# Eight loads of the second half of x tied to the end of the first half's RWKV-7 projections, in a hybrid RWKV-7 / RG-LRU / GLA block

## The chip, the core and the metric

The kernel runs on one core of one Trainium2 chip. The metric is device microseconds of one execution; before the change the median of three runs is 1198.15 us. TensorE (PE) does the matmuls, VectorE (DVE), ScalarE (ACT) and GpSimd (POOL) the elementwise work, and SyncE (SP) only issues DMAs. Each engine takes its instructions strictly in the order in which they stand in its row, so an instruction that waits holds up all that stand behind it.

## The reference, cut to what matters

T = 1024 tokens, width D = 1024, one layer. One combined projection feeds three mixers, whose outputs go through an output projection and then an FFN.

```python
hn = rms_norm(x, norm1_g)                       # x * rsqrt(mean(x*x) + eps) * g
p_rw, p_lru, p_gla = split(hn @ w_in)           # RWKV-7 | RG-LRU | GLA
y_rw  = rwkv7_mixer(p_rw)     # p + (token_shift(p) - p) * mu, then a delta-rule scan
y_lru = rglru_mixer(p_lru)    # causal conv of width 4, gates, a linear recurrence
y_gla = gla_mixer(p_gla)      # chunked gated linear attention, rms_norm * silu(gate)
x = x + concat([y_rw, y_lru, y_gla]) @ w_out
x = x + (silu(rms_norm(x) @ w_gate) * (rms_norm(x) @ w_up)) @ w_down
return rms_norm(x)
```

## The kernel before

All is kept transposed: channels on the 128 partitions, tokens along the free axis. The tokens are taken as two halves of 512 (h = 0 and 1). For each half a tile `y0` or `y1` (128 x 8 x 515) first holds x (eight slices k of 128 channels, in columns 3 to 514) and later the mixers' outputs. Columns 0 to 2 of a slice are room for the convolution's three earlier tokens.

**Projections.** `mm3` computes one projection tile of 128 outputs x 512 tokens with 24 matmuls in one PSUM bank `mm`, of which there are two. Weights come as two pieces `wr` of 256 KB (L120), which ACT and DVE split in a high and a low part (`wh` L104, `wl` L105); both are written back to DRAM (`parts`, L122, L123), so that half 1 loads them instead of making them again. x is split alike into `xh`, `xl`. The result leaves PSUM by DVE L252, which multiplies it with `rstd`, the norm's factor. `proj` can therefore run its matmuls before `rstd` is there, but only as far as there are `mm` banks.

**rstd of half 1** is made by `split_x(1)`: squares of the eight slices of y1 (L225), their sum over channels by one matmul (L174 into a bank `pi`), then on ACT `Ln` (L136) and `Exp` (L137). ACT must load a table (ACT_TABLE_LOAD) each time it goes from `Exp` to `Ln` or back.

**Token shift.** `rw_shift` keeps the last token of each of half 0's eight RWKV-7 projections in a column of `carry` (128 x 8), with one ACT copy each (L276); half 1 takes its first token from there. The eight projections are steps R0 (seven of them) and H0 (the eighth, `pgl`).

**What sets the order.** A list of steps (ORDER) is written out in the program: R0, H0, then pieces of the RWKV-7 chain (a, b, c, p), of GLA (P0, G0), of RG-LRU (l, L) and, in the middle, X1 (`load_x(1)`), S1 (`split_x(1)`) and R1, half 1's projections. A scheduler then merges the steps by priorities (AHEAD lifts some of them) and by its own estimate of when operands are ready, and writes each engine's row for good. A single added dependency can so move rows on all engines.

**Names the prediction uses.** Half 0's GLA step G0 ends with L574 (copies out of PSUM), L584 to L586 (gate), L593, L174 into `px`, twice L595 (`Ln`) and L597 (`Exp`). RG-LRU's step L01 begins beside it with L619, L611, L621 (gate), L628 and L630 (convolution), L634 (matmul into `px`, two banks) and L635 (ACT out of `px`). L455 and L465 are small matmuls of the RWKV-7 chain, L301 and L309 of its preparation.

Of the kernel before, what the change touches and what calls it, by code (L numbers as in the profile page):

```python
# [68 lines left out]
def hybrid_block(tc, xT, vec, cst, w_in, w_gk, w_ups, lru_w, gk_up, w_out, w_gu, w_dn, outT):  # L69
    nc = tc.nc  # L70
    V, G, S, PE = nc.vector, nc.gpsimd, nc.scalar, nc.tensor

    with ExitStack() as ctx:
# [12 lines left out]
        carry = cp.tile([P, 8], F32, name="carry")  # L86
# [125 lines left out]

        def load_x(h, ks=range(NK)):
            x = ys[h]
            for k in ks:
                nc.sync.dma_start(out=x[:, k, 3:], in_=xT[k, :, h * HT : (h + 1) * HT])

# [494 lines left out]
        with tc.high_priority(offset=10000):  # L712
            S.dma_start(out=vt, in_=vec)
            pre = [[load_w(w_in[6, :, 0:4], 6, 0)]]
            load_x(0, range(2))
            with tc.high_priority(offset=-500):
                pre.append([load_w(w_in[2, :, 0:4], 2, 0)])
            load_x(0, range(2, 4))
            with tc.high_priority(offset=-500):
                pre[0].append(load_w(w_in[6, :, 4:8], 6, 1))  # L720
            load_x(0, range(4, NK))
            nc.sync.dma_start(out=ct[:, CST["ones"][0] :], in_=cst[:, CST["ones"][0] :])
            xs = split_x(0)
# [363 lines left out]
        for f in range(PRE, NF):  # L1087
# [5 lines left out]
            h = gate_up(f, f + 1 if f < NF - 1 else None)  # L1093
# [253 lines left out]
```

## Time and profile before

| | |
|---|---|
| median of three runs (lowest, highest) | 1198.15 us (1198.10, 1199.42) |
| the profiled execution, its time | 1197.18 us |
| its span, granted clock of TensorE | 1195.4 us, 0.996 |
| TensorE busy | 1158.2 us (97%) |
| VectorE, ScalarE, GpSimd busy | 817.2 (68%), 558.5 (47%), 179.5 (15%) |
| DMA | 225.52 MB, 189 GB/s over the span |

TensorE is busy for all but some 37 us of the span, so what moves the time is mostly what puts a hole in its row or closes one. The profiled execution is 0.97 us under the median, and 1.8 us of its time lie outside the span.

### The profile page before, as it was taken

What the parts mean: (1) busy time and instruction counts of PE and PEld (TensorE: products, weight loads), DVE (VectorE), ACT (ScalarE), POOL (GpSimd) and SP (SyncE); (2) the same over time, 40 slices, a digit from 0 to 9 for tenths busy, and PEclk for the clock granted to TensorE, in tenths of its full rate; (3) what the DMA queues carried; (4) which work ended last, traced back from release to release, by engine and by line L of the source; (5) the groups of instructions that cost most, each with busy time, mean ns of one, the idle gap of its engine ahead of it and who ended that gap; (6) DMA issues with size and microseconds to landing.
All of it is one profiled execution on the core that took longest, in us unless ns stands there. A gap on an engine that the chain in (4) does not pass through costs nothing.

```text
span 1195.4 us, 18422 instructions
## 1 busy us (share of the span) xinstructions
PE 1158.2 (97%) x6550; PEld 906.2 (76%) x6550; DVE 817.2 (68%) x1513; ACT 558.5 (47%) x972; POOL 179.5 (15%) x141
## 2 busy tenths in 40 slices
PE   8899999999999999988999999999999999999996
PEld 5676667677776777766788788888888878888886
DVE  6878797887759687468978654356665465555675
ACT  7445734864551367546433333333333344444552
POOL 0000000000000000000026544455545400000000
PEclk9999999999999999999999999999999999999998
DMA  9865444253433269783699862245545798665322
GB/s 320 300 223 193 142 148 134 90 158 98 142 109 104 67 206 313 249 312 116 219 337 326 283 213 82 89 132 185 170 152 167 277 358 293 194 194 168 116 98 71
DMA packets 125212, 225.52 MB, mean 189 GB/s; under 512 B 13984, under 2 KB 17344, under 8 KB 125120
## 3 DMA queue, kind: packets, MB, share of 16 engines
q1 hardware_dynamic: 124432, 223.78, 56.0%
q8 instruction: 51, 0.84, 0.3%
q10 hardware_dynamic: 688, 0.57, 0.1%
q14 instruction: 41, 0.34, 0.1%
HBM read 149.84 MB, written 74.45 MB: 188 GB/s over the span
## 4 chain that ended last, share of the span: by engine, by line
PE 65%; DVE 14%; DMA 9%; ACT 8%; issue 3%; SPq 1%; POOL 0%; DVEq 0%; ACTq 0%; POOLq 0%
PE mm L869 24%; PE mm L1132 18%; PE mm L133 15%; DMA wr<-w_gu_dram 3%; DVE x L862 2%; DMA x<-w_dn_dram 2%; PE pi L368 1%; DMA wr<-w_in_dram 1%; DVE ws L862 1%; DMA wd<-x 1%; PE pi L408 1%; ACT L663 1%; DMA parts<-wh 1%; DVE wl L105 1%; DVE x L831 1%
## 5 line engine op out<-in xcount | busy, mean ns | idle before, releaser
L133 PE MATMUL mm<-xl,wh 128*128 128x512 f32 x420 | 168.8, 402 | 0.0
L133 PE MATMUL mm<-xh,wh 128*128 128x512 f32 x400 | 162.6, 407 | 3.9 <-ACT wh L104 3.1
L133 PE MATMUL mm<-xh,wl 128*128 128x512 f32 x400 | 162.9, 408 | 0.3 <-DVE wl L105 0.3
L104 ACT CAST wh<-wr 128x512 fp32r<-128x512 f32 x133 | 82.0, 619 | 123.1 <-PE mm L869 43.4
L104 ACT CAST vh<-wr 128x512 fp32r<-128x512 f32 x81 | 50.2, 622 | 103.7 <-PE mm L1132 39.1
L133 PEld LDWEIGHTS mm<-xl,wh 128*128 128x128 f32 x420 | 78.9, 188 | 21.9 <-issue 6.1
L133 PEld LDWEIGHTS mm<-xh,wh 128*128 128x128 f32 x400 | 75.1, 188 | 26.8 <-issue 5.9
L133 PEld LDWEIGHTS mm<-xh,wl 128*128 128x128 f32 x400 | 75.1, 188 | 22.6 <-issue 5.8
L105 POOL TENSOR_TENSOR wl<-wr,wh 128x512 fp32r<-128x512 f32 x36 | 51.1, 1418 | 268.1 <-DVE x L1042 208.1
L1132 PE MATMUL mm<-ft,vh 128*128 128x512 f32 x264 | 81.5, 389 | 0.0
L1132 PE MATMUL mm<-ft,wh 128*128 128x512 f32 x264 | 81.4, 389 | 0.0
L862 DVE TENSOR_TENSOR x<-x 128x512 f32<-128x512 f32 x71 | 58.7, 834 | 29.5 <-DMA x<-w_dn_dram 16.9
L105 DVE TENSOR_TENSOR wl<-wr,wh 128x512 fp32r<-128x512 f32 x97 | 66.2, 685 | 7.0 <-ACT wh L104 6.6
L417 POOL MEMSET ri<- 128x256 f32 x8 | 2.5, 312 | 390.0 <-DVE ri L402 387.9
L1132 PEld LDWEIGHTS mm<-ft,vh 128*128 128x128 f32 x264 | 49.5, 188 | 10.6 <-DVE ft L105 0.3
L1132 PEld LDWEIGHTS mm<-ft,wh 128*128 128x128 f32 x264 | 49.5, 188 | 10.5 <-DVE ft L105 0.2
L105 POOL TENSOR_TENSOR vl<-wr,vh 128x512 fp32r<-128x512 f32 x36 | 49.5, 1375 | 37.9 <-ACT vh L104 34.9
L1132 PE MATMUL mm<-ft,wl 128*128 128x512 f32 x132 | 51.4, 389 | 0.0
L1132 PE MATMUL mm<-ft,vl 128*128 128x512 f32 x132 | 51.4, 389 | 0.0
L105 POOL TENSOR_TENSOR vl<-ws,vh 128x512 fp32r<-128x512 f32 x27 | 38.3, 1420 | 39.6 <-ACT vh L104 34.8
L104 ACT CAST wh<-ws 128x512 fp32r<-128x512 f32 x33 | 20.4, 622 | 50.9 <-PE mm L869 43.7
L105 POOL TENSOR_TENSOR wl<-ws,wh 128x512 fp32r<-128x512 f32 x27 | 36.9, 1367 | 36.4 <-ACT wh L104 35.0
(501 smaller groups left out, 2898.4 us busy)
## 6 DMA issues: line engine op xcount, KB each, us to landing
wr<-w_gu_dram SPq DMA_DIRECT2D x108, 256.0 KB, 3.1
parts<-wh SPq DMA_DIRECT2D x60, 256.0 KB, 3.3
parts<-wl SPq DMA_DIRECT2D x60, 256.0 KB, 3.0
wh<-parts SPq DMA_DIRECT2D x57, 256.0 KB, 2.7
wl<-parts SPq DMA_DIRECT2D x57, 256.0 KB, 2.9
wr<-w_in_dram SPq DMA_DIRECT2D x44, 256.0 KB, 3.7
x<-w_dn_dram SPq DMA_DIRECT2D x44, 256.0 KB, 4.7
wd<-x SPq DMA_DIRECT2D x44, 256.0 KB, 4.3
```

Of the source, the lines that this page charges most:

```text
L104: S.copy(out=hi, in_=src)
L105: lo_eng.tensor_tensor(out=lo, in0=src, in1=hi.bitcast(F32), op=ALU.subtract)
L133: PE.matmul(out=ps, lhsT=ww[:, kk], rhs=xx(k), start=first, stop=last)
L368: PE.matmul(out=pgs[hh][:, n * P : n * P + P], lhsT=BKn[hs(hh), nn, 64 * hh : 64 * hh + 128], rhs=ARn[hs(hh), nn], start=True, stop=True)
L408: PE.matmul(out=ps[hs(hh), n * w : n * w + w], lhsT=lhs(hh, n), rhs=rhs(hh, n), start=True, stop=True)
L417: G.memset(hi(Zt), 0.0)
L663: S.activation(out=gate, in_=gate, func=AF.Exp, scale=-0.5)
L831: V.scalar_tensor_tensor(out=xk, in0=xk, scalar=vc("g2", k), in1=rs, op0=ALU.mult, op1=ALU.mult)
L862: eng.tensor_tensor(out=out, in0=a, in1=b, op=op)
L869: PE.matmul(out=ps, lhsT=ww[:, kk], rhs=xx, start=first and kk + i == 0, stop=kk == len(xc) - 1 and i == 2, skip_group_check=True)
L1132: PE.matmul(out=out(m), lhsT=ww[:, m], rhs=xx, start=first and open_(m) and k + i == 0, stop=k == KF - 1 and i == 2, skip_group_check=True)
```

## The change

`load_x(h)` for h = 1 gets one ACT copy ahead of its loads. It writes the eight columns of `carry` into column 3 of y1's eight slices. The eight loads then overwrite column 3, among others, with x. What the copy writes is thus never read; but each load must come after the copy, and the copy after the last of the eight writes to `carry`, which is that of step H0. (Line numbers from L216 on are higher by 3 after the change.)

```diff
         def load_x(h, ks=range(NK)):
             x = ys[h]
+            if h:
+
+                S.copy(out=x[:, :, 3], in_=carry)
             for k in ks:
                 nc.sync.dma_start(out=x[:, k, 3:], in_=xT[k, :, h * HT : (h + 1) * HT])
```

On SP's row the eight loads (`y1`, 256 KB each) stood early, among the weights (`wr`) of the first projections and the write-backs (`parts`). Before:

```order
L120 DMA wr<-w_in_dram 128x512
L181 DMA gku<-gk_up_dram 32x128
L216 DMA y_101<-xT_dram 128x512 x2
L189 DMA rt<-w_gk_dram 128x128
L216 DMA y_101<-xT_dram 128x512 x2
L122 DMA parts<-wh 128x512
L216 DMA y_101<-xT_dram 128x512
L123 DMA parts<-wl 128x512
```

After, on the same row, some fifty places further on:

```order
L122 DMA parts_81<-wh_699 128x512
L219 DMA y1_101<-xT_dram 128x512
L123 DMA parts_81<-wl_700 128x512
L120 DMA wr_1014<-w_in_dram 128x512
L219 DMA y1_101<-xT_dram 128x512
L122 DMA parts_81<-wh_719 128x512
L123 DMA parts_81<-wl_720 128x512
L120 DMA wr_1036<-w_in_dram 128x512
L219 DMA y1_101<-xT_dram 128x512 x6
```

All eight loads now stand behind thirteen more weight pieces than before, six of them in one run.

On ACT's row, at the end of GLA's half 0, `rstd` of half 1 is made by L136 and L137. Before (the names with u are work tiles of GLA and RG-LRU):

```order
L595 ACT_TABLE_LOAD
L595 ACTIVATE u_qk<-px,vt 128x512
L628 ACTIVATE u_2311<-y_100,vt 128x512
L619 ACTIVATE u_2304<-ga 128x512
L136 ACTIVATE rstd<-pi,vt 128x512
L137 ACT_TABLE_LOAD
L137 ACTIVATE rstd<-rstd 128x512
L621 ACTIVATE u_2304<-u_2304 128x512
L276 COPY carry<-pw 128x1
L595 ACT_TABLE_LOAD
```

After (L598 is L595 of before, L600 is L597, L622 is L619, L624 is L621, L631 is L628):

```order
L598 ACT_TABLE_LOAD
L598 ACTIVATE u_qk<-px,vt 128x512
L631 ACTIVATE u_2312<-y_100,vt 128x512
L598 ACTIVATE u_qk<-px,vt 128x512
L622 ACTIVATE u_2300<-ga 128x512
L600 ACT_TABLE_LOAD
L600 ACTIVATE u_qk<-u_qk 128x1024
L624 ACTIVATE u_2300<-u_2300 128x512
L136 ACT_TABLE_LOAD
L136 ACTIVATE rstd<-pi,vt 128x512
L137 ACT_TABLE_LOAD
L137 ACTIVATE rstd<-rstd 128x512
```

Both L595, both L621 and L597 now stand ahead of `rstd`, with a table load for L597 and one for L136 between.

On PE's row the third projection tile of half 1 begins at the 577th of the matmuls of L133. It writes the `mm` bank of the first tile, which DVE must have emptied with `rstd`. Before, it followed the second tile (`mm_2415`) at once:

```order
L174 MATMUL px_2145<-u_2_2143,ct_67 128x512
L450 MATMUL pc_2736<-R0_2744,Tt_1812 64x64 x4
L133 MATMUL mm_2415<-xh7_2268,wh_2432 128x512
L133 MATMUL mm_2415<-xl7_2269,wh_2432 128x512
L133 MATMUL mm_2415<-xh7_2268,wl_2433 128x512
L133 MATMUL mm_2454<-xh0_2240,wh_2455 128x512
L133 MATMUL mm_2454<-xl0_2241,wh_2455 128x512
```

After, other work stands between the second tile (`mm_2416`) and the third (`mm_2455`); L637 is L634 of before, L468 is L465 and L458 is L455 (the first rows of that work):

```order
L133 MATMUL mm_2416<-xh7_2269,wl_2434 128x512
L174 MATMUL pi_2296<-rt_2240,ct_67 128x512
L453 MATMUL pc_2737<-R0_2745,Tt_1813 64x64 x4
L637 MATMUL px_2318<-u_0_2312,lw_2310 128x512
L637 MATMUL px_2321<-u_0_2312,lw_2310 128x512
L468 MATMUL pp_2738<-XR0_1714,UV0_1080 64x64
L458 MATMUL pc_2737<-UV0_1080,BKt_1748 64x64
```

and its last rows, with the third tile's first:

```order
L468 MATMUL pp_2738<-XR1_1715,UV1_1081 64x64
L468 MATMUL pp_2738<-XR0_1714,UV0_1080 64x64
L468 MATMUL pp_2738<-XR1_1715,UV1_1081 64x64
L637 MATMUL px_2333<-u_1_2327,lw_2325 128x512
L133 MATMUL mm_2455<-xh0_2241,wh_2456 128x512
```

The three L637 and the L458/L468 group came after the third tile's first matmuls before, and the sum for `rstd` (L174 into `pi`) stood inside the second tile. The chain's small matmuls moved as well: the ends of GLA's scores and sums stand 12 matmuls of L133 later on PE's row than before (the last L578, now L581, after the 17th matmul of the second tile instead of after the 5th), and similar shifts of 12 to 22 run from about the 62nd matmul of L133 to the 570th. From about the 1300th on, and in the whole FFN, PE's row is the same.

## Rows read from the trace of the kernel before

**Rows 1.** Stretches: length, busy PE, PEld, DVE, ACT, POOL, granted clock, DMA share, GB/s.

```profile
18.00:45.00 27.00, 22.61 (x98) 15.63 (x98) 19.02 (x46) 18.44 (x35) 0.00 (x0) 1.00 0.89 318
40.00:60.00 20.00, 19.65 (x91) 15.54 (x92) 19.75 (x54) 5.76 (x13) 0.00 (x0) 1.00 0.88 304
```

**Rows 2.** TensorE's waits, 18 to 60 us: us in total, times, longest.

```profile
PE mm L133 <- ACT wh L104: 3.1, 2, 2.8
PE pi L301 <- ACT pw L279: 0.8, 1, 0.8
PE mm L133 <- DVE wl L105: 0.3, 1, 0.3
PE pi L174 <- ACT rt L320: 0.2, 1, 0.2
```

**Rows 3.** SyncE's queue, 17 to 33 us: start, us, line; last, its loads' landing time.

```profile
17.80 0.96 SPq L216 DMA_DIRECT2D y<-xT_dram  x2
...
23.95 1.62 SPq L120 DMA_DIRECT2D wr<-w_in_dram  x2
25.62 1.43 SPq L216 DMA_DIRECT2D y<-xT_dram  x3
...
y<-xT_dram SPq DMA_DIRECT2D x8, 256.0 KB, 4.8
```

**Rows 4.** TensorE's waits, 60 to 240 us, the three chain waits.

```profile
PE pi L301 <- DVE Tt L426: 1.1, 1, 1.1
PE pi L408 <- DVE ri L420: 1.0, 1, 1.0
PE pi L174 <- DVE rt L341: 0.8, 1, 0.8
```

**Rows 5.** ScalarE in order of time from 213 us: start, us, instruction, wait before it.

```profile
213.44 0.43 ACT L574 COPY u_v<-px 128x128 f32<-128x128 f32 x2 [7.33 <-PE px L572]
...
215.90 0.81 ACT L628 ACTIVATE u<-y,vt 128x512 f32<-128x512 f32 x1 [0.98 <-DVE y L586]
...
217.74 1.28 ACT L595 ACT_TABLE_LOAD   x1
219.03 0.69 ACT L595 ACTIVATE u_qk<-px,vt 128x512 f32<-128x512 f32 x1
...
220.32 0.62 ACT L619 ACTIVATE u<-ga 128x512 f32<-128x512 f32 x1
...
222.83 0.63 ACT L137 ACTIVATE rstd<-rstd 128x512 f32<-128x512 f32 x1
223.37 0.61 ACT L621 ACTIVATE u<-u 128x512 f32<-128x512 f32 x1
...
228.24 1.06 ACT L597 ACTIVATE u_qk<-u_qk 128x1024 f32<-128x1024 f32 x1
```

**Rows 6.** TensorE in order of time, the third tile of half 1 and later.

```profile
224.24 0.50 PE L133 MATMUL mm<-xh,wh 128*128 128x512 f32 x1 [0.82 <-DVE pw L252]
...
227.11 1.02 PE L634 MATMUL px<-u,lw 128*128 128x512 f32 x2
...
228.20 0.40 PE L133 MATMUL mm<-xl,wh 128*128 128x512 f32 x1
228.44 0.39 PE L133 MATMUL mm<-xh,wl 128*128 128x512 f32 x1
...
230.09 0.27 PE L465 MATMUL pp<-XR,UV 128*64 128x64 f32 x1
...
230.75 0.48 PE L301 MATMUL pi<-pw,ups 64*128 64x256 f32 x1
...
269.27 0.68 PE L346 MATMUL pi<-ct,pv 64*64 64x64 f32 x16 [0.16 <-DVE pv L277]
```

**Rows 7.** Stretches at the FFN's start, columns as in rows 1.

```profile
553.00:557.00 4.00, 1.04 (x3) 0.68 (x4) 4.00 (x8) 3.18 (x6) 0.00 (x0) 0.98 0.00 0
557.00:560.20 3.20, 3.20 (x9) 2.42 (x9) 3.20 (x7) 2.94 (x5) 0.00 (x0) 0.50 0.12 9
```

## The prediction, made before the changed kernel was run

> **What bounds the kernel now.** I read the table of busy times first. TensorE is busy for 1158.2 of 1195.4 us, so a change can gain only by closing holes in TensorE's row, some 37 us in all, and loses when it makes new ones. The list of TensorE's waits then says where the holes are. From 18 to 45 us TensorE is busy for 22.61 of 27.00 us, while the DMA engines move 318 GB/s at a share of 0.89 [rows 1]. Its four waits there are 3.1 + 0.8 + 0.3 + 0.2 = 4.4 us [rows 2], nearly all of that gap, and the largest of them, 2.8 us, is for a weight that ACT has yet to split. SyncE's queue shows why the weight is late: the eight loads of y1 are issued from 17.80 to about 27 us, five of them ahead of the weight pieces issued at 23.95 us, and land some 4.8 us after their issue [rows 3]. Half 1's x is not needed there. From 40 to 60 us TensorE is busy for 19.65 of 20.00 us, and VectorE for 19.75 [rows 1]: from there on DMA is no longer what holds TensorE.
>
> The changed order moves most at the place where half 1's norm factor is made, so I last read ScalarE's and TensorE's rows in order of time from 213 to 231 us [rows 5, 6].
>
> **Part 1: the loads leave the early stretch (a gain).** Eight pieces of 256 KB are 2.1 MB, and at 318 GB/s 6.6 us of DMA time. That is the upper end of the gain; the lower end is 0, if the weights turn out to wait for SyncE's issuing or for ScalarE's splitting instead. The nearest rows are the four waits, 4.4 us [rows 2]. Walking the loads out of the queue, the weights behind them land earlier by somewhat more than TensorE waits, and two small matmul groups come later in TensorE's row as well, so that I take **5.0 us**. The loads themselves come later, behind thirteen more weight pieces. I take them to be late for no one: their first readers stand in S1, six steps behind X1 in the list, and no wait of TensorE is for them [rows 2, 4]. The copy (128 x 8) goes beside other work on ScalarE, and its price is nothing that TensorE sees; uncovered it would be no more than the two larger copies of L574, 0.43 us [rows 5].
>
> **Part 2: the order that follows from it (a loss).** The scheduler wrote all rows anew. I sum the new place of `rstd` from one anchor, T0 = 213.44 us, GLA's last copy L574 [rows 5].
>
> Before: `rstd` is done when L137 ends, 223.46 us, T0 + 10.0 [rows 5]. VectorE empties the bank with it, and the third tile's first matmul starts at 224.24 us, T0 + 10.8, after a wait of 0.82 us [rows 6].
>
> After: ScalarE has these more ahead of `rstd`, from start to start as in its rows (neighbours overlap by about 0.05 to 0.1 us) [rows 5]: two L621 at 0.6, one L595 at 0.6, one L619 at 0.55, L597 at 0.97, and two table loads of 1.29 (217.74 to 219.03), in sum 5.9 us. Less the 0.98 us in which ScalarE waited at the first L628, that is 10.0 + 5.9 - 1.0 = 14.9 us of plain occupancy. But L628, L619 and L621 now come sooner on ScalarE than VectorE's work ahead of them; walking both rows with the durations of before, I find waits of 0.7 + 0.5 + 1.5 = 2.7 us. So `rstd` is done at T0 + 17.6. Ahead of the third tile TensorE now also has the third L634, which needs a `px` bank that ScalarE's L635 must free first, and L635 stands behind L137: 0.6 us for L635 and 0.8 for the L634 bring the third tile to T0 + 19.0.
>
> T0 itself comes 12 matmuls later in TensorE's row. A matmul is 0.24 us from start to start (228.20 to 228.44), rounded down to 0.227 for the long runs of them: 2.7 us. And TensorE does work ahead of the third tile that it did behind it before: three L634, each 227.11 to 228.20 less one matmul, 0.86, and the L455/L465 group, 230.09 to 230.75, 0.66 [rows 6], in sum 3.2 us. The loss is 19.0 - 10.8 + 2.7 - 3.2 = **7.7 us**. By plain occupancy alone, without the 2.7 us of waits, it is 5.0. TensorE thus has a hole of some ten microseconds with about 3 us of small work in it.
>
> A second, later hole is possible: L346 stood 0.16 us behind VectorE's L277 at 269.27 us [rows 6], and is now 14 matmuls earlier in the row (699 instead of 713). From 0 to 2 us; I take 0 and keep 2 for the range, so that the loss reaches from 5.0 to 9.7.
>
> What ScalarE's table loads cost is read here from start to start: load at 217.74, the activation that needs it at 219.03, 1.29 us [rows 5]. The Trainium skill ("ScalarE: Activation LUTs", What ACT_TABLE_LOAD costs) puts another 1.38 us of drain on every switch; by it the two added loads would be an estimated 2.8 us dearer, and the forecast 2.8 us higher. The rows show no such gap behind the load, so the sum goes by 1.29.
>
> **Part 3: the clock.** After two near-by holes at the FFN's start (TensorE busy for 1.04 of 4.00 us) the granted clock is 0.50 for 3.20 us, the 1.2 GHz level, and half of that, 1.6 us, is lost [rows 7]. The new hole in part 2 is longer, so I expect the same behind it: **1.6 us**. The lower end is 0: behind the early hole of 2.8 us the granted clock stayed at 1.00 [rows 1, 2]. The upper end is twice the row, 3.2.
>
> **Sum.** -5.0 + 7.7 + 1.6 = +4.3 us against the profiled execution, 1197.18 us: 1201.5. That execution is 0.97 us under the median, so 1202.5 us.
>
> **The rivals.**
>
> *Slack (the other side, faster).* The small matmuls of the chains stand 12 to 22 matmuls later in TensorE's row for most of 60 to 210 us. Their operands then have more time, the three waits of TensorE there, 1.1 + 1.0 + 0.8 = 2.9 us [rows 4], go, and VectorE comes to T0 ahead of ScalarE, so that the loss is plain occupancy, 5.0, with no clock loss since much of the hole has work in it. -5.0 - 2.9 + 5.0 = -2.9: 1195.2 us. For it speaks that these waits are short and single, so that a few matmuls of slack cover them; against it VectorE's 19.75 of 20 us [rows 1]: it is VectorE that the chains wait for, and it does not get faster. It decides if the hole of part 2 stays below 7.9 us, the gain and the three waits together, and the clock at 1.00.
>
> *A draw.* The gain is as forecast, the hole at its lower end, the clock stays up: -5.0 + 5.0 = 0, 1198.2 us. For it speaks that a wait of VectorE's in my walk falls away as soon as VectorE is 3 us early.
>
> *The change doesn't do what it says.* The early weights are held by ScalarE's splitting and not by the loads: 8 pieces fewer change nothing, the gain is 0, and the loss stays: +9.3, 1207.5 us. For it speaks that TensorE's largest wait names ScalarE's `wh` [rows 2]; against it that ScalarE is busy for 18.44 of 27.00 us there and so waits itself, with DMA at 0.89 [rows 1].
>
> **How the numbers follow.** The measurement can tell about 0.2% from no change, 2.4 us here. Forecast 0.52; slack 0.20; draw 0.20; no gain 0.08. Slack is faster by over 0.2%, the draw is the same, the other two are slower: 0.20, 0.20, 0.60. The forecast's own range, from the lower ends of its loss and clock with a gain of 6.6 to the upper ends, holds mostly between 1199 and 1206.5. For 8 in 10 the range takes in the draw and about half of the slack case, and leaves out the no-gain case: 1195.0 to 1206.5 us.
>
> **What would show it.** Part 1: the y1 loads at over 60 us on SyncE's queue, and the wait for `wh` at 32 us gone. Part 2: at about 220 us a hole in TensorE's row that ends with L634 or with the first matmul of the third tile, released by ScalarE's L635 or VectorE's eviction, with L137 ending some 17 us behind the last L574 of that step. Part 3: a stretch of granted clock 0.50 behind it. The prediction is wrong if TensorE reaches the third tile with `rstd` already there, or if TensorE is no earlier at 60 us than before.

## The result: slower by 0.9%, and the profile after

The changed kernel takes 1209.78 us (median of 6), the kernel before 1199.41 us in the same measurement: ratio 1.009, interval [1.0064, 1.0116]. The profiled execution of after has a span of 1205.6 us against 1195.4 us, 10.2 us more, and it is read below.

The page, part 1, of after (engine, busy us, share of the span, instructions):

```profile
PE 1162.7 (96%) x6550; PEld 908.9 (75%) x6550; DVE 816.2 (68%) x1513; ACT 559.4 (46%) x974; POOL 179.7 (15%) x141
```

The work is the same; TensorE has 5.7 us more of holes, and takes 4.5 us more for the same matmuls. First the stretches that answer to [rows 1], with two short ones behind holes (length, busy PE, PEld, DVE, ACT, POOL, granted clock, DMA share, GB/s):

```profile
18.00:45.00 27.00, 27.00 (x117) 20.57 (x116) 19.39 (x38) 18.45 (x36) 0.00 (x0) 1.00 0.94 331
40.00:60.00 20.00, 20.00 (x105) 15.64 (x104) 17.20 (x45) 9.04 (x16) 0.00 (x0) 1.00 0.79 266
...
106.00:110.00 4.00, 1.65 (x33) 1.31 (x34) 4.00 (x6) 0.67 (x2) 0.62 (x2) 0.99 0.38 131
110.00:113.00 3.00, 3.00 (x7) 1.96 (x6) 2.03 (x4) 1.67 (x3) 0.00 (x0) 0.50 0.00 0
...
228.00:232.00 4.00, 3.49 (x4) 1.17 (x4) 2.84 (x6) 3.95 (x5) 0.00 (x0) 0.50 0.00 0
```

From 18 to 45 us TensorE is now busy throughout. SyncE's queue shows the loads of y1 out of the way (start, us, line), against [rows 3]:

```profile
62.20 0.33 SPq L219 DMA_DIRECT2D y<-xT_dram  x1
63.53 0.49 SPq L219 DMA_DIRECT2D y<-xT_dram  x1
65.57 4.23 SPq L219 DMA_DIRECT2D y<-xT_dram  x6
```

TensorE's waits in the three stretches 18 to 60, 60 to 240 and 240 to 300 us (us in total, times, longest); the first answers to [rows 2], the second to [rows 4]:

```profile
PE pi L133 <- DVE xl L236: 0.3, 1, 0.3
...
PE px L637 <- DVE u L633: 5.0, 1, 5.0
PE pi L411 <- DVE ri L405: 1.8, 1, 1.8
PE pi L174 <- DVE rt L344: 1.1, 1, 1.1
PE pc L453 <- DVE R L450: 1.0, 1, 1.0
PE px L174 <- ACT u L658: 1.0, 1, 1.0
PE px L637 <- ACT y L638: 0.9, 1, 0.9
PE pi L304 <- DVE Tt L429: 0.3, 1, 0.3
...
PE pi L174 <- ACT rt L323: 2.0, 1, 2.0
PE pi L349 <- DVE pv L280: 0.8, 1, 0.8
```

The early waits fell from 4.4 us to 0.3, by 4.1. Behind them stand 13.9 us of waits, where before there were 3.9 (the three of [rows 4], the 0.82 and the 0.16 us of [rows 6]). The largest are at the place that the prediction named. ScalarE in order of time there (start, us, instruction, wait before it), against [rows 5]:

```profile
215.42 0.43 ACT L577 COPY u_v<-px 128x128 f32<-128x128 f32 x2 [10.51 <-PE px L575]
...
217.68 0.81 ACT L631 ACTIVATE u<-y,vt 128x512 f32<-128x512 f32 x1 [0.26 <-DVE y L589]
...
219.28 0.63 ACT L622 ACTIVATE u<-ga 128x512 f32<-128x512 f32 x1 [0.78 <-DVE y L589]
...
222.20 0.63 ACT L624 ACTIVATE u<-u 128x512 f32<-128x512 f32 x1 [1.82 <-DVE u L614]
...
232.82 0.63 ACT L137 ACTIVATE rstd<-rstd 128x512 f32<-128x512 f32 x1
233.36 0.67 ACT L638 ACTIVATE y<-px,bah 128x512 f32<-128x512 f32 x1
```

and TensorE there and at the two other new holes, against [rows 6]:

```profile
107.38 1.12 PE L411 MATMUL pi<-ri,XL 64*64 64x32 f32 x32 [1.81 <-DVE ri L405]
109.47 1.66 PE L174 MATMUL px<-u,ct 128*128 128x512 f32 x2 [0.96 <-ACT u L658]
...
228.51 3.75 PE L637 MATMUL px<-u,lw 128*128 128x512 f32 x4 [4.98 <-DVE u L633]
...
234.08 1.12 PE L637 MATMUL px<-u,lw 128*128 128x512 f32 x2 [0.91 <-ACT y L638]
234.64 0.79 PE L133 MATMUL mm<-xh,wh 128*128 128x512 f32 x1
...
254.94 1.13 PE L174 MATMUL pi<-rt,ct 128*128 128x512 f32 x2 [2.04 <-ACT rt L323]
```

So T0, the last copy of GLA, is at 215.42 us, rstd is done at 233.45, T0 + 18.0, and the third tile starts at 234.64, T0 + 19.2. Before, it started at 224.24 [rows 6]. The longest wait in this hole, 5.0 us, is not for rstd but for the convolution (L633 on VectorE, L630 of before), and only the 0.91 us are for L638, which stands behind rstd. That the place of rstd decides all the same is what the experiments show.

### The profile page after: what moved, and what is told of

It reads as the page before. It is cut to its first block, busy times and chain, and to the rows that moved or that the text cites. A ratio compares the mean times of both kernels' runs of the same rounds, so it can differ in the third digit from the quotient of the medians.

```text
span 1205.6 us, 18423 instructions
## 1 busy us (share of the span) xinstructions
PE 1162.7 (96%) x6550; PEld 908.9 (75%) x6550; DVE 816.2 (68%) x1513; ACT 559.4 (46%) x974; POOL 179.7 (15%) x141
## 4 chain that ended last, share of the span: by engine, by line
PE 72%; DVE 13%; DMA 7%; ACT 5%; issue 2%; SPq 1%; DVEq 0%; ACTq 0%
PE mm L872 23%; PE mm L133 19%; PE mm L1135 17%; DMA wr<-w_gu_dram 3%; DVE x L865 2%; DMA x<-w_dn_dram 2%; PE pi L411 1%; PE pi L371 1%; PE px L637 1%; PE pi L133 1%; DVE ws L865 1%; PE px L573 1%; PE px L174 1%; PE pi L174 1%; DVE x L834 1%
## 5 line engine op out<-in xcount | busy, mean ns | idle before, releaser
L133 PE MATMUL mm<-xl,wh 128*128 128x512 f32 x420 | 168.4, 401 | 0.0
L133 PE MATMUL mm<-xh,wh 128*128 128x512 f32 x400 | 162.5, 407 | 0.0
L133 PE MATMUL mm<-xh,wl 128*128 128x512 f32 x400 | 161.2, 404 | 0.0
L104 ACT CAST wh<-wr 128x512 fp32r<-128x512 f32 x133 | 82.2, 618 | 123.3 <-PE mm L872 43.4
L104 ACT CAST vh<-wr 128x512 fp32r<-128x512 f32 x81 | 50.2, 622 | 102.3 <-PE mm L1135 39.2
L133 PEld LDWEIGHTS mm<-xl,wh 128*128 128x128 f32 x420 | 79.2, 189 | 20.2 <-issue 4.3
L133 PEld LDWEIGHTS mm<-xh,wh 128*128 128x128 f32 x400 | 75.5, 189 | 23.0 <-issue 6.8
L133 PEld LDWEIGHTS mm<-xh,wl 128*128 128x128 f32 x400 | 75.4, 189 | 20.7 <-issue 4.6
L1135 PEld LDWEIGHTS mm<-ft,wh 128*128 128x128 f32 x264 | 49.6, 188 | 10.2
L104 ACT CAST wh<-ws 128x512 fp32r<-128x512 f32 x33 | 20.4, 622 | 50.3 <-PE mm L872 41.1
```

The source lines that it names most:

```text
L104: S.copy(out=hi, in_=src)
L133: PE.matmul(out=ps, lhsT=ww[:, kk], rhs=xx(k), start=first, stop=last)
L1135: PE.matmul(out=out(m), lhsT=ww[:, m], rhs=xx, start=first and open_(m) and k + i == 0, stop=k == KF - 1 and i == 2, skip_group_check=True)
```

## The experiments

All twelve change the rows of some engine, so the first thing to look at is where they begin to differ. The table gives the start of the matmul of L133 that has n others of L133 ahead of it (576: the first of the third tile) in each profiled execution, as the difference to the kernel before (us; the times of before are 46.73, 101.49, 210.50, 224.24, 249.74, 472.91 and 528.23). Small matmuls stand at other places among them, so differences of a few us between neighbours mean little; steps that stay do. A profiled execution is one of several: that of e9 is the longest of its nine (1213.16 us, median 1207.30), those of e4 and e10 lie 5 us under their medians, the others within 2.6 us of theirs.

| n | after | e1 | e2 | e3 | e4 | e5 | e9 | e10 | e11 | e12 |
|---|---|---|---|---|---|---|---|---|---|---|
| 120 | -5.9 | -6.2 | 1.0 | 0.5 | -1.3 | -2.6 | -6.3 | -6.8 | -5.7 | -3.9 |
| 312 | -5.2 | -5.6 | 1.0 | 0.5 | -1.3 | -0.1 | -8.2 | -6.1 | -7.6 | -7.8 |
| 552 | -4.8 | -5.2 | 1.1 | 1.1 | -7.3 | 0.4 | -11.5 | -12.6 | -13.9 | -13.1 |
| 576 | 10.4 | -6.6 | 12.7 | 2.5 | 15.6 | 15.6 | 11.5 | 1.1 | -9.2 | -8.4 |
| 648 | 11.8 | -5.0 | 13.8 | 1.5 | 18.3 | 17.0 | 14.0 | 2.0 | -6.4 | -5.6 |
| 1224 | 9.6 | -3.1 | 10.9 | 1.6 | 16.2 | 14.8 | 13.1 | 1.1 | -5.8 | -5.0 |
| 1416 | 11.4 | 6.2 | 20.8 | 16.2 | 16.6 | 16.1 | 15.1 | 1.1 | -5.9 | -4.8 |

### Is it the late rstd or the late data? (e1 to e4)

The theory after the first look: the scheduler's new rows put rstd late on ScalarE, and the hole comes from that ("order"). The rival: y1 lands late and all behind it is late ("late data").

**e1**, late loads, early rstd: the changed kernel with

```diff
-                ps = head_sum(acc, ones, prep_ps if h else mix_ps)
+                ps = head_sum(acc, ones, post_ps if h else mix_ps)
```

> The changed kernel, with the sum for half 1's rstd in the bank pp instead of pi. All rows are those of the changed kernel up to about the 559th matmul of L133, the loads of y1 stay late, but rstd now stands ahead of the last copies of GLA's half 0 on ScalarE. Theory 'order' (the late rstd makes the hole at 220 to 234 us): the third tile of half 1 no longer waits, some 8 us come back of the 10.4: 1199 to 1203 us. Rival 'late data' (y1 lands late and all behind it is late): no change, 1207 to 1210 us.

Measured: 1204.27 us, ratio 1.0056 [1.0038, 1.0073], a little over what was expected. TensorE's rows are those of after up to the 559th matmul of L133. rstd is done ahead of T0 now (ScalarE in order of time):

```profile
210.00 0.63 ACT L137 ACTIVATE rstd<-rstd 128x512 f32<-128x512 f32 x1
...
216.89 0.43 ACT L577 COPY u_v<-px 128x128 f32<-128x128 f32 x2 [3.15 <-PE px L575]
```

The step of 15 us between matmuls 552 and 576 is gone (-5.2 to -6.6), and e1 stays ahead of the kernel before until the 1224th. Then it loses 9 us in 50, ahead of the FFN, in good part to weights that land late (5.6 us, against 2.0 in the kernel before; TensorE's waits of e1, 480 to 560 us):

```profile
PE px L133 <- DMA wh<-parts: 2.7, 2, 2.0
PE mm L133 <- ACT y L104: 1.9, 1, 1.9
PE pi L133 <- DMA wh<-parts: 1.8, 2, 1.0
PE mm L133 <- DMA wh<-parts: 1.1, 2, 0.9
```

**e2**, early loads, late rstd: the kernel before with

```diff
-                ps = head_sum(acc, ones, prep_ps if h else mix_ps)
+                ps = head_sum(acc, ones, mix_ps)
```

> The kernel before, with the sum for half 1's rstd in a bank px instead of pi. All rows are those of before up to about the 559th matmul of L133, the loads of y1 stay early, but rstd now stands behind both L595 and L597 on ScalarE. Theory 'order': a hole of 6 to 9 us ahead of the third tile, without any dependency of the loads: 1204 to 1208 us. Rival 'late data': nothing is late, 1198 to 1200 us.

Measured: 1218.21 us, 1.017 [1.0142, 1.0198]. The hole comes without any dependency of the loads: 1.1 us behind at matmul 552, 12.7 at 576. That is more than expected, and another 10 us are lost behind the 1224th matmul, as in e1.

**e3**, the control, early loads and early rstd: the kernel before with e1's line.

> The control of the first: the kernel before with the sum in pp. Loads early, rstd earlier than before. Theory 'order': the third tile's wait of 0.8 us goes, 1197 to 1199 us; if the bank pp itself costs something, it shows here as 1200 or more. Rival 'late data': as before, 1198 to 1199 us.

Measured: 1215.64 us, 1.0155 [1.0133, 1.0176], where 1197 to 1199 was expected. Up to the 1224th matmul it is near where it should be (1.6 us behind, of which 0.5 since the first 50 us). All the rest, 14.6 us, is lost behind it (TensorE's waits of e3, 480 to 545 us):

```profile
PE pp L488 <- ACT ro L136: 4.3, 1, 4.3
PE px L133 <- DMA wh<-parts: 3.3, 2, 1.9
PE pi L133 <- DMA wh<-parts: 2.4, 2, 1.6
```

So e1 to e3 are read at the 1224th matmul and not at their ends: to use another bank for one sum gives other rows 250 us later, and behind the 1224th matmul 9 to 15 us are lost in all three.

**e4**, the changed kernel whose copy waits for nothing:

```diff
-                S.copy(out=x[:, :, 3], in_=carry)
+                S.copy(out=x[:, :, 3], in_=vt[:, 0:8])
```

> The changed kernel, with the copy reading a constant tile that is there from the start instead of carry, so that the loads wait for nothing and stand as early on SyncE's queue as before. The scheduler still writes the rows anew, with rstd behind both L598 and L600. Theory 'order': the hole at 220 us is there and there is no early gain: 1206 to 1212 us. Rival 'late data': like before, 1198 to 1200 us.

Measured: 1217.24 us, 1.0161 [1.0124, 1.0199], 5 us over the expected range. With the loads early but rows of the new kind the kernel is slower than the changed one: the late rstd is there (a step of 22.9 us between 552 and 576) and the early gain is not. Data that come early do not help. With e6 below, where data that come later still do not hurt, "late data" is out.

### What are the late loads worth by themselves? (e5, e6)

**e5**: the loads wait for the first projection tile alone.

```diff
-                S.copy(out=x[:, :, 3], in_=carry)
+                S.copy(out=x[:, :, 3], in_=carry[:, 6:7].to_broadcast([P, NK]))
```

> The changed kernel, with the copy reading only the column of carry that the first projection tile writes. The loads of y1 stand about 35 places earlier on SyncE's queue, among the weights again; all other rows are nearly those of the changed kernel (194 of TensorE's 5509 differ). Theory 'gain kept': the early stretch loses the 4 to 6 us again that the late loads gave, and all behind it is later by that: 1211 to 1216 us. Rival 'gain spent by the chain anyway' (TensorE waits for the chain at 105 us whatever it gained): the hole at 105 us shrinks by the same, 1208 to 1210 us as with the change.

Measured: 1214.96 us, 1.0149 [1.0106, 1.0192]. SyncE's queue, TensorE's waits from 18 to 60 us, and T0 on ScalarE:

```profile
25.85 1.93 SPq L219 DMA_DIRECT2D y<-xT_dram  x4
...
34.01 0.33 SPq L219 DMA_DIRECT2D y<-xT_dram  x1
```

```profile
PE mm L133 <- ACT wh L104: 3.3, 1, 3.3
PE mm L133 <- DVE wl L105: 0.5, 1, 0.5
```

```profile
220.62 0.43 ACT L577 COPY u_v<-px 128x128 f32<-128x128 f32 x2 [10.51 <-PE px L575]
```

With the loads among the weights the wait for `wh` is back, and T0 is at 220.62 us, 5.2 us behind after's. TensorE's rows of the two differ almost only from 37 to 84 us (by after's time). From there they run in step: 5.2 us apart at matmuls 312, 552, 576, 648 and 1224. This is the value of the late loads in nearly the same order, **5.2 us**, and it is kept to the end. But it is not all waiting. The two waits are 3.8 us, and behind them e5 has a lowered clock (columns as above):

```profile
43.00:50.00 7.00, 5.41 (x12) 3.86 (x13) 6.85 (x18) 2.31 (x6) 0.00 (x0) 0.51 0.66 235
```

TensorE is busy there for 5.41 us at 0.51, which costs some 2.7 us. The kernel before had waits of 4.4 us in its early stretch and a granted clock of 1.00 [rows 1, 2]. So the 5.2 us are not what the loads cost in it, and T0 of e5, 220.62 - 213.44 = 7.2 us later than before the change, holds more than the price of the new order.

**e6**: the loads wait for a value of RG-LRU's second tile; TensorE's row is the very same as after's.

```diff
-                S.copy(out=x[:, :, 3], in_=carry)
+                S.copy(out=x[:, :, 3], in_=lhalo[:, 1, 0:1].to_broadcast([P, NK]))
```

> The changed kernel, with the copy reading a value that RG-LRU's second tile writes, so that the loads of y1 stand some 25 places later still on SyncE's queue; TensorE's row is the very same. Theory 'order': 1207 to 1211 us like the change, since nothing waits for y1. Rival 'late data': slower by what they come later, several us, 1213 us or more.

Measured: 1210.7 us, 1.0099 [1.0073, 1.0126], not to be told from the change (1.009). The loads go out at 86 to 94 us and nobody waits for them.

### Other ways to an early rstd (e7, e8)

**e7**: the sum in a projection bank.

```diff
-                ps = head_sum(acc, ones, prep_ps if h else mix_ps)
+                ps = head_sum(acc, ones, (lambda: pm.tile([P, HT], F32, name="mm")) if h else mix_ps)
```

> The changed kernel, with the sum for half 1's rstd in a bank mm. rstd stands ahead of GLA's last copies on ScalarE, as with bank pp, but a projection bank is held for it. Theory 'order': no hole of rstd at 220 us, so 1198 to 1205 us; the bank held costs up to 2 us. Rival 'late data': 1207 to 1210 us.

Measured: 1217.95 us, 1.0158 [1.0133, 1.0184], a miss. The hole at 220 us is gone here too (7.9 us ahead of before at matmul 576), but the rows behind lose it: 3.4 us ahead at the 648th, 3.4 behind at the 1224th, 25.8 behind at the 1416th, with a single wait of 11.1 us, for the split of y at L104, ahead of the FFN.

**e8**: as e1, and the later sum for the FFN's norm of half 0 in bank pp too.

```diff
-                rsqrt_exp(acc, head_sum(acc, ones, prep_ps), 1.0 / D, vc("eps6"))
+                rsqrt_exp(acc, head_sum(acc, ones, post_ps), 1.0 / D, vc("eps6"))
```

> As the first experiment (late loads, half 1's sum in pp), and the sum for the FFN's norm of half 0 in pp too, which gives other rows behind about the 1250th matmul of L133. The first experiment was 2 to 4 us ahead of before up to there and lost 8 us in the next 30 us to weights that came late. Theory: if that loss is of the rows there, it changes with them, 1196 to 1202 us; if it is what late loads cost in the end, it stays: 1202 to 1206 us.

Measured: 1204.32 us, 1.0054 [1.0034, 1.0074]. It is at -3.2 us at the 1224th matmul like e1 and loses 8 us behind it too, in other rows. By the expectation this speaks for the late loads as the cause; against that, e3 loses 14.6 us there with early loads, and the changed kernel only 1.8 with late ones. The test did not decide what that loss belongs to.

### The hole at 105 us (e9 to e12)

On VectorE's row of after the chain's transposes (L405) stand behind RG-LRU's scan (L654) and its neighbours, and TensorE waits for them. VectorE in order of time, after:

```profile
103.91 1.28 DVE L654 TENSOR_TENSOR_SCAN u<-y,lstate,u 128x512 f32<-128x512 f32 x1
105.11 0.67 DVE L653 TENSOR_TENSOR u<-u,u 128x512 f32<-128x512 f32 x1
105.69 0.68 DVE L105 TENSOR_TENSOR wl<-wr,wh 128x512 fp32r<-128x512 f32 x1
106.30 1.03 DVE L405 STREAM_TRANSPOSE ri<-ri 128x512 f32<-128x512 f32 x1
```

and before, the same transpose:

```profile
102.53 0.68 DVE L611 SCALAR_TENSOR_TENSOR u<-u,u 128x512 f32<-128x512 f32 x1
103.13 1.08 DVE L402 STREAM_TRANSPOSE ri<-ri 128x512 f32<-128x512 f32 x1
```

TensorE's projections are 5.2 us earlier at this point (matmul 312), and the chain is 3.2 us *later*.

**e9**: the changed kernel with RG-LRU's first mixing step at a lower priority.

```diff
-    "a0": 5060, "b0": 3000, "a1": 2000, "L00": 1000, "c0": 2250,
+    "a0": 5060, "b0": 3000, "a1": 2000, "L00": -500, "c0": 2250,
```

> The changed kernel with RG-LRU's first mixing step (L00) at a lower priority. On VectorE's row the chain's transposes (L405) now stand ahead of RG-LRU's scan (L654); rstd stays behind L598 and L600. Theory 'two holes': the hole at 105 us with the lowered clock behind it (some 4.5 us) goes, the one at 220 us stays: 1203 to 1207 us. Rival 'one hole' (all of the loss is the late rstd, and what is gained at 105 us is waited for at 220): 1208 to 1211 us.

Measured: 1207.3 us, 1.007 [1.005, 1.0091], against 1.009 of the change: not to be told apart. The transpose is at 100.35 us and TensorE has no hole from 100 to 120 us. But GLA's end now stands behind 576 matmuls of L133 on TensorE's row (569 in after, 557 before), T0 comes at 216.62 us, and the late rstd takes back what was gained: -11.5 us at matmul 552, +11.5 at 576. The median lies between the two expected ranges and decides for neither.

**e10**: the same priority at 300.

```diff
-    "a0": 5060, "b0": 3000, "a1": 2000, "L00": 1000, "c0": 2250,
+    "a0": 5060, "b0": 3000, "a1": 2000, "L00": 300, "c0": 2250,
```

The transposes still stand behind the scan; rstd is early, in its old bank.

> The changed kernel with step L00 at a slightly lower priority: the chain's transposes still stand behind the scan, but rstd is made ahead of the second L598, as before the change, in its old bank. Theory 'two holes': the hole at 220 us goes (6 to 8 us), the one at 105 us stays: 1200 to 1204 us. Rival 'the bank did it' (the first experiment gained because pp was used): 1208 to 1211 us.

Measured: 1205.78 us, 1.0038 [1.0011, 1.0065] (its runs spread from 1196.8 to 1209.2), between the two expected ranges. In the profiled execution T0 is at 214.25 us and the third tile, TensorE in order of time, at T0 + 11.1:

```profile
225.35 0.80 PE L133 MATMUL mm<-xh,wh 128*128 128x512 f32 x1 [0.32 <-DVE pw L255]
```

With rstd early and bank pi it is 1.1 us behind before's, not 10.4: it was not the bank. A new wait of 4.3 us, of L468 for VectorE's copy L454, stands there instead.

**e11**: e1 and e9 together, both holes closed.

```diff
-    "a0": 5060, "b0": 3000, "a1": 2000, "L00": 1000, "c0": 2250,
+    "a0": 5060, "b0": 3000, "a1": 2000, "L00": -500, "c0": 2250,
...
-                ps = head_sum(acc, ones, prep_ps if h else mix_ps)
+                ps = head_sum(acc, ones, post_ps if h else mix_ps)
```

> Late loads, the chain's transposes ahead of the scan, and rstd early in the bank pp. Theory 'two holes': both are gone and the early gain is left: 1193 to 1199 us. Rival: the loss comes back in the last 100 us ahead of the FFN, as in the first experiment: 1200 to 1206 us.

Measured: **1191.21 us, 0.9922 [0.9892, 0.9951]**, faster than both kernels and than expected. The stretches of e11 (columns as above) show TensorE without the hole at 105 us and nearly without the one at 220, at full clock:

```profile
100.00:120.00 20.00, 20.00 (x191) 14.32 (x190) 9.99 (x17) 7.95 (x11) 0.62 (x2) 1.00 0.43 142
200.00:240.00 40.00, 38.95 (x361) 27.65 (x360) 32.76 (x66) 25.84 (x44) 0.70 (x2) 1.00 0.30 97
```

and its rows behind the 1224th matmul happen not to lose anything (-5.8, then -5.9 us).

**e12**, its control: e11 with e4's copy, that is with the loads early.

```diff
-                S.copy(out=x[:, :, 3], in_=carry)
+                S.copy(out=x[:, :, 3], in_=vt[:, 0:8])
```

> The control of the eleventh: the same kernel, with the copy reading a constant tile, so that the loads of y1 wait for nothing and go early again; TensorE's rows are the same but for some 200 between the 96th and the 400th matmul. Theory 'gain kept': the late loads are worth what they were in the fifth experiment, some 5 us, so 1194 to 1198 us. Rival 'all from the rows': 1189 to 1193 us, as in the eleventh.

Measured: 1193.53 us, 0.9966 [0.9953, 0.9978], between the two expected ranges. By the ratios the late loads are worth 0.4% in this order too, with intervals that just do not meet; in the two profiled executions e12 loses 1.8 us by matmul 120, gets it back by 312, stays about 1 us behind e11 up to the 1416th, and has the shorter span in the end (1189.5 us against 1190.5). So most of what makes e11 faster than before is its order; what the loads add is not settled, between nothing and some 5 us.

## Why the prediction was wrong in size

The sign, the place and the mechanism were forecast; the size was +4.3 us, measured +10.2 us in the span and +10.4 in the medians, outside the range. The "no gain" rival's 1207.5 us comes nearest to the 1209.78 measured, by chance: its premise, a gain of 0, did not hold. By its steps:

- **Early gain, 5.0: right in kind, some 0.9 too large.** The waits for the weights went [rows 2]: 4.1 us. The 5.2 of e5 agree with the forecast in part by luck, for they hold the loss of a lowered clock that the kernel before did not have. That VectorE's full row at 40 to 60 us [rows 1] would spend it was not so.
- **rstd on ScalarE, T0 + 17.6, and the third tile at T0 + 19.0: right.** Measured 18.0 and 19.2. The waits for VectorE that the walk put at 2.7 us are 0.26 + 0.78 + 1.82 = 2.9 us. Each added table load costs 1.29 us from start to start, as in [rows 5]; the estimate from the drain that the Trainium skill ("ScalarE: Activation LUTs", What ACT_TABLE_LOAD costs) states would have put rstd at T0 + 20.4, 2.4 us too late.
- **T0, "12 matmuls later: 2.7 us": the step that failed.** T0 is 2.0 us later than before, although 4.1 us of early waits had gone, so the term was 6.1 us and 3.4 short. (e5 gives 7.2, with a clock loss of its own in it.) The prediction counted what TensorE does ahead of T0, and that count is right: the traces have 1415 instructions there against 1403, the twelve matmuls of L133 more and nothing else. But it took the chain's operands to be there in time. They are not: from 60 us to T0 TensorE waits 1.8 + 1.1 + 1.0 + 0.3 = 4.2 us, against 2.9 before [rows 4], 1.3 more; and behind the hole at 107 us the granted clock is 0.50 for 3 us, 1.5 us lost. Of the other 0.6 us, 0.5 are there already at matmul 60 (24.55 us before, 25.04 after). The rival "slack" rested on the same error with its sign turned: chain matmuls that stand later on TensorE's row did not have more time, because what feeds them stands later on VectorE's row too (L405, 106.30 against 103.13).
- **The second, later hole, 0 taken of 0 to 2: mis-sized.** At the place that it named (L346, now L349, at 275.92 us) the wait is 0.8 us, where before it was 0.16 [rows 6]. Another one, L174 at 254.94 us with 2.0 us, was not foreseen. Together +2.7 us.
- **The clock, 1.6 behind the hole at 220: there, but free.** The stretch from 228 to 232 us has a granted clock of 0.50, but the four L637 that it slows would have waited for rstd and L638 anyway. The loss of 1.5 us came behind the other hole, at 110 us, and is counted in T0 above.

With the measured terms, and the 3.2 us of work moved ahead as the prediction had it: -4.1 + (19.2 - 10.8 + 6.1 - 3.2 = 11.3) + 2.7 = +9.9 us, against 10.2 in the spans.

Why does a lone repair bring so little, while both together bring 18 us against the change? At the 1224th matmul after is at +9.6 us, e1 at -3.1 and e11 at -5.8: by there the early rstd brings 12.7 us and the repair of the other hole 2.7 more. e1 then loses 9 us behind it and e11 nothing. e9's gain is waited for at the late rstd, as its rows show. What stays open: e1, e2, e3 and e8 lose 8 to 15 us behind the 1224th matmul, e7 22, and e11 does not; which of their rows does it was not tried.

## What to carry to other kernels

Where a scheduler writes the rows of all engines, a dependency is not a local edit: its own effect (here 4 to 5 us gained) was nearly as computed, and the rewritten order cost about three times that. So check in the new rows, ahead of any gain, what stands in front of each producer that the bottleneck engine waits for, on the producer's own engine; moving a consumer later gives no slack if its producer has moved too. And a control that keeps the order (e5, e6) is worth more than one that keeps the idea (e3, e4), if its granted clock is read as well (e5).

## What was not expected of the hardware

Two holes of TensorE of 1.8 and 1.0 us, with 32 small matmuls between, were enough for 3 us at the 1.2 GHz level behind them (after, 110 to 113 us). And one and the same hole does not always have the same effect. The hole of 2.8 us at 30 us left the clock at 1.00 in the profiled execution of the kernel before [rows 1, 2]. e2 and e3 have the same rows there and a hole of 2.7 and 2.8 us; the stretch behind it in before, e2 and e3:

```profile
33.00:36.00 3.00, 2.80 (x11) 1.84 (x11) 1.82 (x6) 1.01 (x2) 0.00 (x0) 1.00 0.89 331
33.00:36.00 3.00, 3.00 (x6) 1.41 (x5) 1.48 (x3) 0.41 (x2) 0.00 (x0) 0.50 0.99 346
33.00:36.00 3.00, 3.00 (x5) 1.78 (x6) 1.40 (x5) 0.16 (x1) 0.00 (x0) 0.50 0.83 277
```

So the lower end of the prediction's part 3, no loss behind a hole of 2.8 us, rested on one execution. In the six runs of the changed kernel the mean granted clock goes from 0.992 to 0.982 and the time with it, from 1207.4 to 1215.9 us; where the clock fell in the other five is not on record.
